# Low parts of every sixth weight granule by an accumulating DMA instead of a VectorE subtraction

## Chip, cores and metric

One core of a Trainium2 chip. The metric is the device time of one execution in microseconds (us), the median of three runs. A profile is one further execution with the hardware profiler on.

## What is computed

Two blocks of a hybrid network on 256 tokens of width 2048, all in float32: a convolution and sliding-window attention layer, then an indexer-selected attention layer and a stick-breaking attention layer, each with layer norms and gates. What matters here is that nearly all of it is products of 256 tokens with large weight matrices:

```python
proj = jnp.einsum("bsd,de->bse", x, w_in) + b_in                 # 2048 x 5376
y = jnp.einsum("bse,ed->bsd", y, w_out) + b_out                  # 2048 x 2048
h = x @ w_in_a                                                   # 2048 x 6224
(o * silu(g)) @ w_out_a ;  x @ w_ple_gate ;  p @ w_ple           # twice the last two
kb, vb = split(x @ w_kv_b) ;  q, g = split(x @ w_q_b)            # 2048 x 4096 each
(o * silu(g)) @ w_out_b
```

## The kernel before

Each weight matrix is cut into column chunks, each chunk into granules of 128 partitions x 1024 floats (512 KB; some are 768, 672 or 512 wide): four K-tiles of 256 columns or two of 512. `_plan()` fixes the order of all chunks, and `plan` the order of all 492 granules. For accuracy every float32 operand is split into a high part `hi`, rounded to float32r, and a low part `lo = raw - hi`. A product is then three products of parts: `gemm_T` (weights stationary, lines 338 and 339) takes `hi` against both parts of the activations in one 512-column matmul and `lo` against the high part in a 256-column one; `gemm` (activations stationary, lines 324 to 326) does the three one after the other.

A granule goes through four engines. `load` (lines 250 to 266) issues its DMA on SP's queue into the pool `wraw` of 6 buffers. `fetch` (268 to 278) has ScalarE (ACT) copy it to `hi` with rounding (line 277, the CAST rows), then VectorE (DVE) subtract (line 278, TENSOR_TENSOR); `hi` and `lo` come from the pools `whi` and `wlo` of 4 buffers each. `granules` (292 to 312) sets how far ahead this is written: when granule `here` is being multiplied, `hi` and `lo` of the next `AHEAD` = 2 are written and the next `LOAD` = 3 are loaded. A scheduling layer then orders each engine's instructions, within what buffers and data allow, so that ACT and DVE work further ahead than that. Each engine works its own queue in order. A `raw` buffer is free again when the subtraction has read it.

Attention, convolution and norms run beside this as generators (`side.pump()`, once per granule): small matmuls between the large ones, and ACT, DVE and GpSimd (POOL) work. POOL has little: masks (`affine_select`, line 231 and 1035) and two small DMAs (lines 831 and 835).

```python
            for p in plan[here:here + 1 + min(here, AHEAD)]:
                if p not in held:
                    held[p] = fetch(p)
```

Of the kernel before, what the change touches and what calls it, by code (L numbers as in the profile page):

```python
# [13 lines left out]
F32 = mybir.dt.float32  # L14
F32R = mybir.dt.float32r
I32 = mybir.dt.int32
AF = mybir.ActivationFunctionType
ALU = mybir.AluOpType
# [10 lines left out]
TAPS = 31  # L29
AHEAD = 2  # L30
LOAD = 3
PRE = 3
CONV_RATE = (3, 3)
BIG = 1e30
# [76 lines left out]
def _plan():  # L111

    w2 = [("w_in_a_2", key) for key in CHUNKS_2]
    parts = (("w_kv_b_2", "k", "xy"), ("w_q_b_2", "q", "xy"), ("w_kv_b_2", "v", ("",)), ("w_q_b_2", "g", "xy"))
    w3 = [(w, f"{n}{c}{h}") for c in range(4) for w, n, hs in parts for h in hs]
    square = lambda w: [(w, key) for key in CHUNKS_SQ]
    return [
        *[("w_in", key) for key in CHUNKS_1], *[("w_out", key) for key in CHUNKS_O1],
        ("w_ple0", "0"), ("w_ple0", "1"), *w2, *square("w_out_a_2"),
        ("w_ple0", "2"), ("w_ple0", "3"), *square("w_gate0"), *w3, *square("w_out_b_2"),  # L120
        *[("w_ple1", str(c)) for c in range(4)], *square("w_gate1"),
    ]


def _cols(ranges):
    return sum(n for _, n in ranges)


def _group(ranges, kts):

    if ranges == CHUNKS_1["gv0"][0]:
        return 1
    return min(len(kts), 4 if _cols(ranges) <= 256 else 2)
# [51 lines left out]
def tile_net(ctx: ExitStack, tc: tile.TileContext, t: dict, out: bass.AP):  # L185
    nc = tc.nc
# [5 lines left out]
    wraw = ctx.enter_context(tc.tile_pool(name="wraw", bufs=6))  # L192
    whi = ctx.enter_context(tc.tile_pool(name="whi", bufs=4))
    wlo = ctx.enter_context(tc.tile_pool(name="wlo", bufs=4))
    small = ctx.enter_context(tc.tile_pool(name="small", bufs=4))
    acc = ctx.enter_context(tc.tile_pool(name="acc", bufs=2, space=bass.MemoryType.PSUM))
    aux = ctx.enter_context(tc.tile_pool(name="aux", bufs=4, space=bass.MemoryType.PSUM))
# [5 lines left out]
    def uid(s):  # L203
        count[0] += 1
        return f"{s}_{count[0]}"

    def unit(shape=(P, 2, 512), dt=F32):

        return units.tile(list(shape), dt, tag="u", name=uid("u"))
# [20 lines left out]
    def keep(ap, base, cm, step, op, fill):  # L230
# [10 lines left out]
    held = {}  # L241
    plan = [
        (stream, key, g)
        for stream, key in _plan()
        for kts in (STREAMS[stream][key],)
        for g in range(0, len(kts[1]), _group(*kts))
    ]
    at = [0]

    loaded = {}  # L250

    def load(stream, key, g):

        ranges, kts = STREAMS[stream][key]
        n = _cols(ranges)
        kpg = _group(ranges, kts)
        src = t[stream]
        raw = wraw.tile([P, kpg * n], F32, tag="raw", name=uid("raw"))
        nc.sync.dma_start(
            raw,  # L260
            bass.AP(
                tensor=src.tensor, offset=src.offset + offsets[stream][key] + g * P * n,
                ap=[[kpg * n, P], [1, kpg * n]],
            ),
        )
        return raw

    def fetch(p, keep=False):

        raw = loaded.pop(p, None) or load(*p)  # L270
        shape = list(raw.shape)
        if keep:
            hi, lo = unit(shape, F32R), unit(shape, F32R)
        else:
            hi = whi.tile(shape, F32R, tag="hi", name=uid("whi"))
            lo = wlo.tile(shape, F32R, tag="lo", name=uid("wlo"))
        nc.scalar.copy(hi, raw)  # L277
        return hi, lo, nc.vector.tensor_tensor(lo, raw, hi.bitcast(F32), ALU.subtract)  # L278

    def prefetch(*wanted):  # L280

        for stream, key, count in wanted:
            kpg = _group(*STREAMS[stream][key])
            for g in range(0, count * kpg, kpg):
                p = (stream, key, g)
                if p not in held and plan.index(p) >= at[0]:
                    held[p] = fetch(p, True)
                yield
                yield

    def granules(stream, key, events):

        ranges, kts = STREAMS[stream][key]
        n = _cols(ranges)
        kpg = _group(ranges, kts)
        for g in range(0, len(kts), kpg):
            if events and g in events:
                events[g]()
            here = at[0]
            assert plan[here] == (stream, key, g)  # L300
            for p in plan[here:here + 1 + min(here, AHEAD)]:
                if p not in held:
                    held[p] = fetch(p)
            for p in plan[here:here + 1 + min(here, LOAD)]:
                if p not in held and p not in loaded:
                    loaded[p] = load(*p)
            hi, lo, pace = held.pop((stream, key, g))
            at[0] += 1
            for j in range(kpg):
                ws = slice(j * n, (j + 1) * n)  # L310
                yield kts[g + j], g + j == 0, g + j == len(kts) - 1, hi[:, ws], lo[:, ws]
            with tc.issue_after(pace.ins):
                side.pump()

    def gemm(stream, key, act, events=None):

        n = _cols(STREAMS[stream][key][0])
        both = acc.tile([P, 2, 512], F32, tag="acc", name=uid("acc"))
        ps = [both[:, tt, :] for tt in range(2)]
        for kt, first, last, wh, wl in granules(stream, key, events):  # L320
            for tt in range(2):
                ah, al = act(kt, slice(tt * P, (tt + 1) * P))
                o = ps[tt][:, :n]
                nc.tensor.matmul(o, ah, wh, start=first, stop=False)  # L324
                nc.tensor.matmul(o, ah, wl, start=False, stop=False)  # L325
                nc.tensor.matmul(o, al, wh, start=False, stop=last)  # L326
        return [p[:, :n] for p in ps]

    def gemm_T(stream, key, act, events=None):

        nf = _cols(STREAMS[stream][key][0]) // P
        ps = [acc.tile([P, 2, 2, S], F32, tag="acc", name=uid("acc")) for _ in range(nf // 2)]
        for kt, first, last, wh, wl in granules(stream, key, events):
            both, ah = act.both(kt), act(kt, slice(0, S))[0]
            for f in range(nf):
                o = ps[f // 2][:, f % 2]
                fs = slice(f * P, (f + 1) * P)
                nc.tensor.matmul(o, wh[:, fs], both, start=first, stop=False)  # L338
                nc.tensor.matmul(o[:, 0, :], wl[:, fs], ah, start=False, stop=last)  # L339
        return ps  # L340
# [419 lines left out]
    for c, (s, n) in enumerate(SPANS):  # L760
# [7 lines left out]
        if c == 0:  # L768
            ple[0] = Ple(0)
            side.add(prefetch(("w_ple0", "0", 1), ("w_ple0", "1", 1), ("w_in_a_2", "i0", PRE)), 1, "fetch")  # L770

    def block_end(i, yact, w_out, pre, final):

        ln = Norm(1 + i, z, t["ln_g_2"], t["ln_b_2"], i * D)
        for c, (s, n) in enumerate(SPANS):
# [7 lines left out]
            if c == 0:  # L783
                if i not in ple:
                    ple[i] = Ple(i)
                side.add(
                    prefetch(*[(f"w_ple{i}", str(p), 1) for p in pre], (f"w_gate{i}", "0", PRE)), 1, "fetch"
                )
# [378 lines left out]
```

## Time and profile before

| | us |
|---|---|
| median of 3 runs | 1455.53 (1455.53 to 1456.15) |
| the profiled execution | 1454.93 |
| its span, first to last instruction | 1453.2 |

The profiled execution is 0.60 below the median; 1.73 of its time lies around its span. The TensorE clock was granted at 0.999 of full speed. DMA moved 266 MB, 183 GB/s on average.

To read a profile like this, first look at which engine is busy over the whole span, then at what that engine waits for when it does not work. Work on the other engines counts only as far as that engine waits for it. A busy share is an average over stages, so the windows of the stages come next, and then the distance, in time, between an operand's being ready and its first use.

### The profile page before, as it was taken

What the parts mean: (1) busy time and instruction counts of PE and PEld (TensorE: products, weight loads), DVE (VectorE), ACT (ScalarE), POOL (GpSimd) and SP (SyncE); (2) the same over time, 40 slices, a digit from 0 to 9 for tenths busy, and PEclk for the clock granted to TensorE, in tenths of its full rate; (3) what the DMA queues carried; (4) which work ended last, traced back from release to release, by engine and by line L of the source; (5) the groups of instructions that cost most, each with busy time, mean ns of one, the idle gap of its engine ahead of it and who ended that gap; (6) DMA issues with size and microseconds to landing.
All of it is one profiled execution on the core that took longest, in us unless ns stands there. A gap on an engine that the chain in (4) does not pass through costs nothing.

```text
span 1453.2 us, 21296 instructions
## 1 busy us (share of the span) xinstructions
PE 1437.5 (99%) x8076; PEld 1243.4 (86%) x8076; DVE 1033.6 (71%) x1588; ACT 803.4 (55%) x1199; POOL 24.3 (2%) x51
## 2 busy tenths in 40 slices
PE   7999999999999999999999999999999999999998
PEld 6888888888997888888898898888888888889888
DVE  6999989998679966766758655555655555575754
ACT  6445778465545556646544445654655646554442
POOL 0000000000000000000000000100100001000000
PEclk9999999999999999999999999999999999999999
DMA  8755445556374655455764555555555555586462
GB/s 314 263 197 175 159 138 168 188 191 219 97 240 149 203 165 170 152 182 152 261 196 150 184 174 189 166 175 184 171 174 174 174 175 164 182 269 218 125 223 73
DMA packets 79798, 266.01 MB, mean 183 GB/s; under 512 B 9408, under 2 KB 10048, under 8 KB 79696
## 3 DMA queue, kind: packets, MB, share of 16 engines
q1 hardware_dynamic: 79632, 264.63, 56.3%
q8 instruction: 63, 1.03, 0.3%
q14 instruction: 39, 0.32, 0.1%
q0 software_dynamic: 64, 0.03, 0.0%
HBM read 262.53 MB, written 2.10 MB: 182 GB/s over the span
## 4 chain that ended last, share of the span: by engine, by line
PE 90%; DVE 6%; DMA 2%; issue 1%; ACT 1%; DVEq 0%; SPq 0%; ACTq 0%
PE acc L338 28%; PE acc L339 14%; PE acc L324 14%; PE acc L326 14%; PE acc L325 14%; DVE wlo L278 2%; DVE u L510 2%; DMA raw<-in_w_in 1%; PE o L603 1%; PE pt L384 1%; PE pT L579 1%; PE o L604 0%; DVE u L449 0%; DMA h<-in_ln_b 0%; PE z L1063 0%
## 5 line engine op out<-in xcount | busy, mean ns | idle before, releaser
L278 DVE TENSOR_TENSOR wlo<-raw,whi 128x1024 fp32r<-128x1024 f32 (+3 forms) x475 | 564.0, 1191 | 315.4 <-ACT whi L277 314.7
L277 ACT CAST whi<-raw 128x1024 fp32r<-128x1024 f32 (+3 forms) x475 | 485.8, 1026 | 518.8 <-PE acc L338 244.8
L338 PE MATMUL acc<-u,whi 128*128 128x512 f32 x2016 | 718.3, 400 | 7.7 <-DVE u L378 5.7
L339 PE MATMUL acc<-u,wlo 128*128 128x256 f32 x2016 | 566.9, 281 | 0.0
L338 PEld LDWEIGHTS acc<-u,whi 128*128 128x128 f32 x2016 | 379.4, 188 | 101.5 <-ACT whi L277 5.6
L339 PEld LDWEIGHTS acc<-u,wlo 128*128 128x128 f32 x2016 | 382.0, 189 | 0.3 <-DVE wlo L278 0.3
L324 PE MATMUL acc<-whi,u 128*128 128x512 f32 (+3 forms) x1004 | 358.7, 357 | 0.0
L325 PE MATMUL acc<-wlo,u 128*128 128x512 f32 (+3 forms) x1004 | 355.8, 354 | 0.5 <-DVE wlo L278 0.5
L326 PE MATMUL acc<-whi,u 128*128 128x512 f32 (+3 forms) x1004 | 355.5, 354 | 0.0
L324 PEld LDWEIGHTS acc<-whi,u 128*128 128x128 f32 x1004 | 189.7, 189 | 25.4 <-issue 1.7
L326 PEld LDWEIGHTS acc<-whi,u 128*128 128x128 f32 x1004 | 189.7, 189 | 25.3 <-DVE u L378 0.4
L325 PEld LDWEIGHTS acc<-wlo,u 128*128 128x128 f32 x1004 | 189.9, 189 | 24.4 <-DVE wlo L278 0.9
L510 DVE SCALAR_TENSOR_TENSOR u<-u,convw,u 128x255 f32<-128x255 f32 (+19 forms) x240 | 109.3, 466 | 3.9
L352 DVE TENSOR_TENSOR h<-acc,h 128x512 f32<-128x512 f32 x51 | 34.9, 685 | 5.5 <-ACT h L346 4.6
L467 DVE TENSOR_TENSOR u<-u,h 128x1024 f32<-128x1024 f32 x24 | 28.5, 1220 | 3.4 <-DMA h<-in_ln_g 3.4
L1035 POOL TENSOR_SCALAR_AFFINE_SELECT h<-h 128x256 f32<-128x256 f32 x32 | 18.1, 566 | 748.0 <-DVE h L1055 723.6
L377 ACT CAST u<-h 128x512 fp32r<-128x512 f32 (+1 forms) x32 | 18.0, 566 | 22.0 <-DVE h L616 15.6
L559 ACT ACTIVATE u<-u,negm 128x128 f32<-128x128 f32 x64 | 28.4, 446 | 2.6 <-DVE negm L551 2.6
L378 DVE TENSOR_TENSOR u<-h,u 128x512 fp32r<-128x512 f32 (+1 forms) x32 | 19.7, 622 | 13.9 <-ACT u L377 13.6
L346 ACT ACTIVATE h<-acc 128x512 f32<-128x512 f32 x42 | 24.9, 594 | 5.1 <-PE acc L339 3.8
L803 DVE TENSOR_TENSOR h<-h,u 128x512 f32<-128x512 f32 (+1 forms) x20 | 10.8, 582 | 20.8 <-ACT h L802 20.8
L277 ACT CAST u<-raw 128x1024 fp32r<-128x1024 f32 (+1 forms) x17 | 17.3, 1015 | 11.0 <-DMA raw<-in_w_ple 6.1
(197 smaller groups left out, 965.3 us busy)
## 6 DMA issues: line engine op xcount, KB each, us to landing
raw<-in_w_in_a SPq DMA_DIRECT2D x80, 512.0 KB, 3.6
raw<-in_w_in SPq DMA_DIRECT2D x76, 512.0 KB, 3.3
raw<-in_w_gate SPq DMA_DIRECT2D x64, 512.0 KB, 3.6
raw<-in_w_kv_b SPq DMA_DIRECT2D x64, 512.0 KB, 3.3
raw<-in_w_q_b SPq DMA_DIRECT2D x64, 512.0 KB, 3.3
raw<-in_w_out SPq DMA_DIRECT2D x32, 512.0 KB, 3.4
raw<-in_w_out_a SPq DMA_DIRECT2D x32, 512.0 KB, 4.2
raw<-in_w_out_b SPq DMA_DIRECT2D x32, 512.0 KB, 4.3
```

Of the source, the lines that this page charges most:

```text
L277: nc.scalar.copy(hi, raw)
L278: return hi, lo, nc.vector.tensor_tensor(lo, raw, hi.bitcast(F32), ALU.subtract)
L324: nc.tensor.matmul(o, ah, wh, start=first, stop=False)
L325: nc.tensor.matmul(o, ah, wl, start=False, stop=False)
L326: nc.tensor.matmul(o, al, wh, start=False, stop=last)
L338: nc.tensor.matmul(o, wh[:, fs], both, start=first, stop=False)
L339: nc.tensor.matmul(o[:, 0, :], wl[:, fs], ah, start=False, stop=last)
L346: nc.scalar.activation(t, ps[:, :, 1, :], AF.Copy, scale=scale)
L352: nc.vector.tensor_tensor(out_, ps[:, :, 0, :], t, ALU.add)
L467: nc.vector.tensor_tensor(self.z[c], self.z[c], r.unsqueeze(1).broadcast_to([P, 2, 512]), op)
L510: nc.vector.scalar_tensor_tensor(o[:, d:], h[:, :S - d], w, o[:, d:], ALU.mult, ALU.add)
L559: nc.scalar.activation(sc[:, i, cs], sc[:, i, cs], AF.Exp, bias=negm[:, i, tt:tt + 1], scale=-1.0, accum_out=den[:, i, tt:tt + 1],)
```

## The change

Of the granules of the plan, those with a number over 60 that divides by six, in the second half of their chunk (`g >= 8`), not within the last eight and not of `w_ple`, are `far`: 33 of the 492 (numbers 66, 78, 90, 132, 138, 156, 162, 168, 180, 192, ... 480). For a far granule `hi` and `lo` come from a pool of their own, `wfar`, with one buffer each. ACT writes `hi` by a copy and then (or first) `lo = -raw`, rounded to float32r, by an activation with scale -1. In place of the subtraction, POOL issues a DMA from `raw` to `lo`, SBUF to SBUF, that adds: `lo = raw - hi`. It is fetched 4 granules ahead in place of 2, and loaded 6 ahead in place of 3.

```diff
@@ -29,6 +29,7 @@
 AHEAD = 2
 LOAD = 3
+FAR, FAR_LOAD, FAR_STEP = 4, 6, 6
@@ -192,6 +193,7 @@
     wlo = ctx.enter_context(tc.tile_pool(name="wlo", bufs=4))
+    wfar = ctx.enter_context(tc.tile_pool(name="wfar", bufs=1))
@@ -265,12 +267,23 @@
+    def far(p):
+
+        i = plan.index(p)
+        return i > 60 and i % FAR_STEP == 0 and i < len(plan) - 8 and not p[0].startswith("w_ple") and p[2] >= 8
+
     def fetch(p, keep=False):
 
         raw = loaded.pop(p, None) or load(*p)
         shape = list(raw.shape)
         if keep:
             hi, lo = unit(shape, F32R), unit(shape, F32R)
+        elif far(p):
+            hi = wfar.tile(shape, F32R, tag="hi", name=uid("fhi"))
+            lo = wfar.tile(shape, F32R, tag="lo", name=uid("flo"))
+            nc.scalar.copy(hi, raw)
+            nc.scalar.activation(lo, raw, AF.Copy, scale=-1.0)
+            return hi, lo, nc.gpsimd.dma_start(lo.bitcast(F32), raw, accum_op=ALU.add)
         else:
             hi = whi.tile(shape, F32R, tag="hi", name=uid("whi"))
             lo = wlo.tile(shape, F32R, tag="lo", name=uid("wlo"))
@@ -298,11 +311,11 @@
             here = at[0]
             assert plan[here] == (stream, key, g)
-            for p in plan[here:here + 1 + min(here, AHEAD)]:
-                if p not in held:
+            for i, p in enumerate(plan[here:here + 1 + FAR]):
+                if p not in held and (i <= min(here, AHEAD) or far(p)):
                     held[p] = fetch(p)
-            for p in plan[here:here + 1 + min(here, LOAD)]:
-                if p not in held and p not in loaded:
+            for i, p in enumerate(plan[here:here + 1 + FAR_LOAD]):
+                if p not in held and p not in loaded and (i <= min(here, LOAD) or far(p)):
                     loaded[p] = load(*p)
```

The order of TensorE's matmuls stays as it was, but for a few transposes near granule 290. ACT's changes. This is ACT's queue at granule 322 in the stick-breaking stage, before: `whi_1630` is the high part of granule 322, `whi_1633` of 323, and the rows of lines 1066, 1071 and 609 are attention.

```order
L277 CAST whi_1630_9215<-raw_1623_9184 128x1024
L1071 CAST h_1615_9149<-h_1614_9146 128x256
L1066 ACTIVATE h_1619_9174<-z_1593_9046 128x384
L1071 CAST h_1620_9177<-h_1619_9174 128x256
L609 CAST u_1626_9208<-acc_1573_8959 128x512
L277 CAST whi_1633_9237<-raw_1632_9219 128x1024
```

And after the change, from the row that follows the same `whi_1630` on (lines after 312 are 13 higher); the row that follows the last one is the cast of `whi_1633`.

```order
L1079 ACTIVATE h_1614_9169<-z_1586_9036 128x384
L1084 CAST h_1615_9172<-h_1614_9169 128x256
L1079 ACTIVATE h_1619_9197<-z_1596_9075 128x384
L1084 CAST h_1620_9200<-h_1619_9197 128x256
L284 CAST fhi_1653_9381<-raw_1647_9337 128x1024
L285 ACTIVATE flo_1654_9382<-raw_1647_9337 128x1024
L1079 ACTIVATE h_1624_9225<-z_1603_9107 128x384
L622 CAST u_1626_9231<-acc_1573_8981 128x512
```

The two parts of far granule 330 (`fhi_1653`, `flo_1654`) now stand between the casts of granules 322 and 323, seven granules before their own place. Six of the 33 stand right behind the cast of the granule eight places before them like this one, nine behind that of the seventh before them, seven elsewhere, and eleven (90, 138, 162, 168, 234, 276, 348, 354, 444, 450, 480) behind that of the second before them, most of these because they wait for the single buffer of a far granule six places before.

This is SP's queue after the change, from the load of granule 326 (`raw_1641`) on: the load of far granule 330 (`raw_1647`) stands behind that of 327 and ahead of those of 328, 329 and 331. Before, these were in the order of their numbers.

```order
L261 DMA raw_1641_9308<-in_w_q_b_2 128x1024
L261 DMA raw_1646_9335<-in_w_q_b_2 128x1024
L261 DMA raw_1647_9337<-in_w_kv_b_2 128x1024
L261 DMA raw_1650_9359<-in_w_kv_b_2 128x1024
L261 DMA raw_1655_9386<-in_w_kv_b_2 128x1024
L261 DMA raw_1663_9433<-in_w_kv_b_2 128x1024
```

The far granule's load moved up by two places; it takes the buffer that the subtraction of granule 322 frees, and that load was granule 328's before.

This is POOL's queue after the change near granules 348 to 354, one of the places where the new DMAs stand among the masks of an attention group; `flo_1770` is far granule 354, and the AFFINE_SELECT rows on both sides of it followed each other directly before.

```order
L286 DMA flo_1728_9846<-raw_1719_9794 128x1024
L1048 AFFINE_SELECT h_1732_9870<-h_1732_9870 128x256
L1048 AFFINE_SELECT h_1739_9902<-h_1739_9902 128x256
L286 DMA flo_1770_10039<-raw_1759_9982 128x1024
L1048 AFFINE_SELECT h_1745_9932<-h_1745_9932 128x256
L1048 AFFINE_SELECT h_1753_9966<-h_1753_9966 128x256
```

The third and fourth mask of the group now stand behind a DMA that waits for ACT.

## Rows read from the trace of the kernel before

**Rows 1.** The page's first part: engine, busy us (share of span) xinstructions.

```profile
PE 1437.5 (99%) x8076; PEld 1243.4 (86%) x8076; DVE 1033.6 (71%) x1588; ACT 803.4 (55%) x1199; POOL 24.3 (2%) x51
```

**Rows 2.** Waits of TensorE: engine line <- releaser: us in total, times, longest.

```profile
PE acc L338 <- DVE u L378: 5.7, 1, 5.7
PE acc L338 <- DVE h L352: 2.0, 1, 2.0
PE pt L384 <- DVE h L352: 1.2, 1, 1.2
PE acc L324 <- DVE u L460: 0.5, 2, 0.3
PE acc L325 <- DVE wlo L278: 0.5, 1, 0.5
PE pt L384 <- ACT h L455: 0.3, 1, 0.3
```

**Rows 3.** Waits of the other engines, same columns.

```profile
DVE wlo L278 <- ACT whi L277: 314.7, 271, 3.5
...
ACT whi L277 <- PE acc L338: 244.8, 169, 2.8
ACT whi L277 <- PE acc L326: 226.2, 157, 7.2
```

**Rows 4.** TensorE's timeline, two stretches: start us, us, engine, line, operation.

```profile
879.85 0.39 PE L338 MATMUL acc<-u,whi 128*128 128x512 f32 x1
...
899.96 0.39 PE L338 MATMUL acc<-u,whi 128*128 128x512 f32 x1
...
971.23 0.40 PE L338 MATMUL acc<-u,whi 128*128 128x512 f32 x1
...
979.71 0.40 PE L338 MATMUL acc<-u,whi 128*128 128x512 f32 x1
```

**Rows 5.** Groups by form on DVE, then ACT: busy us, mean ns | idle before.

```profile
L278 DVE TENSOR_TENSOR wlo<-raw,whi 128x1024 fp32r<-128x1024 f32 x438 | 534.0, 1222 | 295.8 <-ACT whi L277 295.2
...
L277 ACT CAST whi<-raw 128x1024 fp32r<-128x1024 f32 x438 | 459.0, 1051 | 484.9 <-PE acc L338 242.4 <-PE acc L326 195.6 <-issue 25.3
```

**Rows 6.** Windows: stretch, length, busy us of PE, PEld, DVE, ACT, POOL, clock, DMA share, GB/s.

```profile
440.00:480.00 40.00, 39.49 (x208) 30.50 (x208) 37.22 (x86) 19.05 (x30) 1.81 (x2) 1.00 0.50 158
...
960.00:1000.00 40.00, 40.00 (x235) 35.05 (x234) 21.52 (x22) 20.58 (x25) 0.00 (x0) 1.00 0.53 173
```

**Rows 7.** DMA issues by line: count, KB each, median us from issue to landing.

```profile
raw<-in_w_kv_b SPq DMA_DIRECT2D x64, 512.0 KB, 3.3
...
raw<-in_w_out_b SPq DMA_DIRECT2D x32, 512.0 KB, 4.3
...
u<-in_x SPq DMA_DIRECT2D x8, 256.0 KB, 7.4
...
h<-in_inv POOLq DMA_DIRECT2D x1, 32.0 KB, 1.9
```

**Rows 8.** ACT's timeline at the casts of granules 322 and 323.

```profile
936.58 1.05 ACT L277 CAST whi<-raw 128x1024 fp32r<-128x1024 f32 x1
...
940.39 1.05 ACT L277 CAST whi<-raw 128x1024 fp32r<-128x1024 f32 x1
941.34 0.49 ACT L1066 ACTIVATE h<-z 128x384 f32<-128x384 f32 x1
```

**Rows 9.** DVE's timeline there: the subtraction of granule 322.

```profile
937.66 1.23 DVE L278 TENSOR_TENSOR wlo<-raw,whi 128x1024 fp32r<-128x1024 f32 x1 [0.94 <-ACT whi L277]
```

**Rows 10.** POOL's timeline near granule 350: the third mask of the group.

```profile
1027.16 0.41 POOL L1035 TENSOR_SCALAR_AFFINE_SELECT h<-h 128x256 f32<-128x256 f32 x1 [3.08 <-DVE h L1055]
```

**Rows 11.** TensorE's timeline there: attention products behind granule 348 and before 351.

```profile
1026.67 0.34 PE L1063 MATMUL z<-h,negtri 128*128 128x384 f32 x1
...
1033.33 0.34 PE L1063 MATMUL z<-h,negtri 128*128 128x384 f32 x1
```

## The prediction

> **What bounds the kernel now.** The page's first part comes first: TensorE is busy 1437.5 of 1453.2 us, DVE 71%, ACT 55%, POOL 2% [rows 1]. A busy TensorE could still be waiting inside its modelled ends, so the second view is its waits: they add up to 10.2 us, of which 7.7 are the two waits on L338 [rows 2]. The largest of these, 5.7 us for an activation, is the start of the kernel, ahead of any weight work that changes. On the line that this change takes work from, DVE's subtraction, TensorE waited once, 0.5 us. The third view says why: ACT's casts wait 471 us for TensorE to give a `whi` buffer back, and DVE's subtractions 315 us for ACT's casts [rows 3]. The supply of weights is held back by TensorE, not the other way round. The fourth view is TensorE's pace: 58 pairs of matmuls between 879.85 and 899.96 are 0.347 us a pair, 24 pairs between 971.23 and 979.71 are 0.353 [rows 4]. A granule of eight pairs is thus 2.8 us, and there are two paces, 2% apart, with no wait in them.
>
> The margin follows from this. A cast starts when TensorE is done with the granule four places before, so three granules (3 x 2.8 = 8.4) are left; the cast takes 1.05 and the subtraction 1.22 [rows 5], so low parts are ready about 6.1 us before use. In the indexer stage DVE is busy 37.2 of 40 us against 21.5 of 40 in a later one [rows 6], and the margin is thinner there.
>
> **The change, part by part.** All of it is off TensorE's queue; a term counts only where it uses up a margin.
>
> *Removed:* 33 subtractions, 33 x 1.22 = 40 us of DVE [rows 5]. DVE is not waited for but for 0.5 us, so this gives at most 0.5 us, in the crowded stage. I take all of it: -0.5. The waits on L352, L460 and L455 are norms and projections, which do not move.
>
> *Added on ACT:* 33 negations. No row shows one; the cast of the same tile, same engine, is 1.05 us [rows 5], so about 35 us on an engine that is 45% idle. By itself: 0.
>
> *ACT's order.* This is where a cost can arise. At granule 330 the far cast and negation stand between the casts of 322 and 323. The far load can start only when the subtraction of 322 has freed its buffer: that one ends at 937.66 + 1.23 = 938.9 [rows 9]. A 512 KB load lands 3.3 to 4.3 us later [rows 7], at 942.2 to 943.2, and ACT, working in order, stands still until then. Cast and negation take 2.1, the two attention instructions behind them about 1.1 (0.49 [rows 8] and one a little longer), so the cast of 323 starts at 945.4 to 946.4 in place of 940.39 [rows 8]: 5 to 6 us late against a margin of 6.1. Six far granules stand like this. The nine behind the seventh cast before them lose about one granule's time less, some 3 us, which the margin covers; after that ACT catches up at about 1 us a granule. If the load lands at 3.3 the cost is nothing. If it takes as long as the slowest kind of load here, 7.4 us [rows 7], the cast is 9.1 us late, 3.0 over the margin, six times: 18 us. Most loads are near the first figure; I take 0.3 us each: +1.8.
>
> *The adding transfer.* POOL issues 33 of them, each up to 512 KB from SBUF to SBUF. The trace has no such operation. From below: POOL's own 32 KB transfer lands in 1.9 us, a 512 KB load in 3.3 [rows 7]; it can hardly be quicker than the load. From above: the slowest kind of load, 256 KB in 7.4 us [rows 7], so 14.8 for 512 KB. An addition has to read `raw` and `lo` and write `lo`, twice the reading of a load; two loads of 3.6 plus issuing make 8 us, and I take 8, nearer the row of equal size. Against it stands the time left: for the 22 far granules written early that is more than 15 us. For the eleven written behind the second cast before them it is five granules, 14.0, less that cast and one or two operations of ACT: 10.9 to 11.9 us. At 8 us nothing is late: 0. At 14.8 each of the eleven is late by about 2.9: 32 us.
> For such a transfer from POOL's queue the Trainium skill (DMA: Bandwidth & Descriptors, Anatomy of one DMA) has a fit of 2.0 us plus bytes over 436 GB/s, which makes 3.2 us here as an estimate, or 4.4 with the bytes read twice. With that the sum would be the same and the margin wider. No run here shows it.
>
> *SP and `raw`.* A far `raw` is held until the transfer has landed, not until a subtraction has read it, so a load that takes its buffer, and SP's queue behind it, wait some 8 us longer than for a subtraction. The six buffers let loads land several granules before their casts; at 8 us this is covered, at 13 or more it adds to the late case.
>
> *POOL's order.* At granule 354 the third mask, at 1027.16 before [rows 10], stands behind a DMA that waits for a negation, and that waits for TensorE to end granule 348, about 1026.7 [rows 11]. Negation 1.05, the attention's own logarithm, a DVE step, the mask and the steps behind it (each 0.4 to 0.7, with the far cast of 1.05 between) end near 1030.5; the product that needs them starts at 1033.33 [rows 11]. 2.8 us in hand: 0. If issuing took longer than that, the cover is gone there.
>
> Sum: -0.5 + 1.8 = +1.3 on 1454.93 of the profiled execution, 1456.2; the median of the runs stood 0.6 above that execution, so **1456.8**. About 0.2%, 2.9 us, is what a measurement of this kernel can tell from no change, so this is "the same".
>
> **The rivals.**
>
> *The transfer is late (slower).* One mechanism: TensorE stands at the first matmul with a far `lo`. It decides from about 11 us from issue to landing. At 13 us it is eleven times 1.1 to 2.1, some 18 us, 1473; at 14.8 us 1488. For it: no row shows an adding transfer, the queue is shared with loads that keep the DMA engines half busy [rows 6]. Against it: every 512 KB row lands within 4.3.
> The Trainium skill (SBUF — State Buffer, Who interferes with whom) says that a DMA issued by GpSimd can be held up while DVE runs a copy, cast or one-input arithmetic in its two-port mode, because the descriptors are written through a port that the two share. That speaks against this change; it would lengthen the time from issue to landing. In rows, DVE's largest group is TENSOR_TENSOR [rows 5], which is not of that kind, so I leave this rival's chance nearly as it is. Chance 0.17.
>
> *ACT's detour costs more (slower).* As priced, a far load of 5 us or more in the six places: at 5 us 0.6 each, and a few us in the crowded stage at granule 180, where the margin is thinner; 4 to 10 us in all, 1460 to 1466. It decides where the cast behind the detour is over 6.1 us late. For it: the arithmetic above ends within a microsecond of the margin. Chance 0.20.
>
> *TensorE's pace changes (faster).* The two paces differ by 0.0067 us a pair, and there are 2016 pairs. If small waits at far granules, or other timing of the small matmuls between, put more stretches into the quicker pace, up to 13.4 us come back if all were slow now; 2.9 us need 440 pairs. Against it: the order of the matmuls stays, and nothing in the diff aims at this. 1450 to 1452. Chance 0.15, and 0.02 more that DVE's relief is worth more than its waits show.
>
> *The change does less than it says:* a far granule's work is only moved and nobody waits. That is the sum without its last term, 1455, inside "the same", 0.03.
>
> **How the numbers follow.** Forecast 0.43; with the last rival 0.46 for the same. Slower 0.17 + 0.20 = 0.37, faster 0.17. The likeliest case alone runs from 1453.5 to 1458.4. The range reaches down to 1451, which leaves out about 0.05 of the quicker pace, and up to 1471, which takes in the detour and leaves out the later half of the late transfers, about 0.1.
>
> **What would show it.** In the profile after: DVE's group on the subtraction smaller by 33 and its busy time near 994 us; ACT's near 838; 33 DMAs on POOL's queue landing in about 8 us; TensorE's waits still near 10 us with at most a few tenths on `flo`. A TensorE wait on `flo` of more than 3 us in all, with landings over 11 us, is the first rival. ACT waiting for a far `raw` for 3 us or more and TensorE then waiting for a `wlo` two to four granules later is the second. A time under 1452.6 with no wait gone and pairs at 0.347 in stretches that were at 0.353 is the third. The forecast is wrong if TensorE's waits grow by more than 3 us or the pace of its pairs shifts.

## The result: 7.8 us slower, and the profile after

The changed kernel takes 1463.62 us (median of 4 runs, 1461.64 to 1465.31) against 1455.84 before: ratio 1.0052, 95% interval 1.0040 to 1.0065. That is slower by more than the 0.2% that a measurement can tell. It lies inside the predicted range, but by luck: the upper part of the range stood for late transfers and for ACT's detour, and neither is what made this time. The likeliest case, 1456.8 and no difference, did not come.

The page's first part, with the same columns as [rows 1]:

```profile
PE 1442.7 (99%) x8076; PEld 1245.8 (85%) x8076; DVE 992.9 (68%) x1555; ACT 827.8 (57%) x1232; POOL 50.7 (3%) x84
```

The work moved as the diff says: DVE has 33 instructions and 41 us less, ACT 33 more and 24 us more, POOL issues 33 DMAs. (Neighbouring instructions overlap by about 0.1 us on ACT and count once, so its busy time grew by less than 33 x 1.05.) The span grew by 8.9 us, TensorE's busy time by 5.2. So some of the loss is waiting, and some is TensorE working more slowly. Its waits after, columns as in [rows 2] (lines of the changed kernel are 13 higher from line 312 on):

```profile
PE acc L351 <- DVE u L391: 5.8, 1, 5.8
PE ix L940 <- ACT h L943: 4.7, 1, 4.7
PE acc L351 <- DVE h L365: 2.0, 1, 2.0
PE acc L337 <- DVE u L473: 0.5, 2, 0.3
PE pt L397 <- ACT h L468: 0.3, 1, 0.3
PE pt L397 <- DVE u L817: 0.3, 1, 0.3
```

One large row is new: a single wait of 4.7 us at the index product L940, for an ACT operation (0.3 us at L397 for `u` is new too). The 0.5 us on DVE's subtraction and 1.2 us near the start (L384 before, at 113 us) are gone. Nothing waits for `flo`. In all the waits grew from 10.2 to 13.6 us. The groups of the new instructions (busy us, mean ns | idle before, by releaser), and two rows of the DMA issues (count, KB, median us to landing):

```profile
L284 ACT CAST fhi<-raw 128x1024 fp32r<-128x1024 f32 (+1 forms) x33 | 34.1, 1033 | 16.7 <-DMA raw<-in_w_q_b 8.0
L285 ACT ACTIVATE flo<-raw 128x1024 fp32r<-128x1024 f32 (+1 forms) x33 | 34.6, 1047 | 6.4 <-PE acc L338 6.4
L286 POOL DMA_DIRECT2D flo<-raw x33 | 28.9, 876 | 1105.1 <-ACT flo L285 976.1
```

```profile
raw<-in_w_kv_b SPq DMA_DIRECT2D x64, 512.0 KB, 3.9
...
flo<-raw POOLq DMA_DIRECT2D x31, 512.0 KB, 5.2
```

The adding transfer lands in 5.2 us in the median, well within its time. To find where the loss is, the start of each TensorE matmul is compared with the start of the matmul of the same number before (the order is the same but for a few small transposes). The difference in us, at times of the trace before, for this kernel and for those of the experiments below:

```
time before    after   e11    e2    e9    e1   e10    e5    e6
        120    +1.01 +1.07 +0.39 +1.71 +1.78 +3.64 +1.43 +0.89
        420    +1.10 +1.13 +0.34 +1.68 +2.15 +3.71 +1.47 +0.97
        450    +8.44 +9.39 +5.94 +2.51 +2.15 +3.71 +1.48 +0.97
        480    +7.63 +8.59 +5.13 +2.78 +1.42 +2.91 +0.67 +0.16
        510    +7.63 +8.49 +5.03 +2.77 +2.51 +2.91 +0.71 +0.06
        end    +8.69 +8.25 +5.37 +2.83 +2.97 +3.76 +0.88 +0.60
```

The first microsecond or more lies ahead of 120 us, where no far granule has been used; e6, which has none at all, shows it too. The loss is one step of 7.3 us between 420 and 450; behind it the column moves by a microsecond at most, as that of e6 does. The timelines show how it comes about. SP's queue there, before and then after (start us, us, grouped; a row lasts as long as SP stands at it):

```profile
418.05 0.33 SPq L259 DMA_DIRECT2D raw<-in_w_in_a  x1
418.43 0.43 SPq L405 DMA_DIRECT2D h<-in_ln_g  x1
```

```profile
415.48 11.78 SPq L261 DMA_DIRECT2D raw<-in_w_in_a  x4
427.31 1.43 SPq L418 DMA_DIRECT2D h<-in_ln_g  x1
```

The four raw loads take 11.78 us in which SP mostly stands. SP's waits in the window from 415 to 445 name what it stood for, and the tile `flo` from 415 to 430 how long that transfer took:

```profile
SPq L261 <- DMA flo<-raw: 7.3, 1, 7.3
```

```profile
DMA to landing us min/median/max: 7.7/7.7/7.7
```

This is the load of granule 159. It takes the buffer that the raw weights of far granule 156 hold until their adding transfer, issued at 419.19, has landed. Behind it in SP's queue stand four norm rows (gain and shift, issued by `row()`). They are issued 8.9 us later than before (1.1 of it because TensorE was already that far behind). Before, DVE waited 0.22 us for the first of these rows, so they had no slack (in brackets the idle time before and what ended it):

```profile
424.02 1.23 DVE L467 TENSOR_TENSOR u<-u,h 128x1024 f32<-128x1024 f32 x1 [0.22 <-DMA h<-in_ln_g]
```

Then DVE, ACT and TensorE, after, one timeline each:

```profile
425.26 1.23 DVE L291 TENSOR_TENSOR wlo<-raw,whi 128x1024 fp32r<-128x1024 f32 x1 [0.30 <-ACT whi L290]
432.39 1.22 DVE L480 TENSOR_TENSOR u<-u,h 128x1024 f32<-128x1024 f32 x1 [5.91 <-DMA h<-in_ln_g]
```

```profile
440.50 1.05 ACT L290 CAST whi<-raw 128x1024 fp32r<-128x1024 f32 x1 [6.14 <-DVE h L365]
444.48 0.62 ACT L984 CAST u<-h 128x512 fp32r<-128x512 f32 x1 [2.93 <-DVE h L892]
445.00 0.40 ACT L988 COPY h<-h 128x256 f32<-128x256 f32 x1
445.31 1.62 ACT L943 ACTIVATE h<-ix 128x384 f32<-128x384 f32 x4
```

```profile
440.87 0.28 PE L352 MATMUL acc<-u,flo 128*128 128x256 f32 x1
445.84 0.96 PE L940 MATMUL ix<-kiT,u 64*128 64x128 f32 x3 [4.70 <-ACT h L943]
...
447.80 0.79 PE L351 MATMUL acc<-u,whi 128*128 128x512 f32 x1
```

DVE stands 5.91 us for a norm row, ACT then stands for DVE, and TensorE for ACT, which has to read earlier index products (`h<-ix`) first. The last row shows the second part of the loss: a matmul of 128x512 takes 0.79 us, not 0.40. The windows (length, PE busy, granted clock, DMA share, GB/s) say why:

```profile
436.00:441.00 5.00, 5.00 (x32) 1.00 0.92 358
441.00:443.00 2.00, 0.15 (x2) 1.00 0.76 274
...
444.00:446.00 2.00, 0.16 (x1) 0.56 0.23 94
446.00:451.00 5.00, 5.00 (x18) 0.50 0.80 239
451.00:456.00 5.00, 5.00 (x28) 0.99 0.85 184
```

The granted clock falls to 0.50, the 1.2 GHz level, at 444.3, still within the wait, and is back at 1.00 at 451.1. In the 5.2 us of this that lie behind the wait TensorE does about half its work: 18 matmuls in 5 us from 446, against 32 in the 5 us ahead of the wait. Half of 5.2 is 2.6 us, and with the wait of 4.7 that is the step of 7.3.

### The profile page after: what moved, and what is told of

The parts are those of the page before. It is cut to its first block, busy times and chain, and to the rows that moved or that the text cites. A ratio compares the mean times of both kernels' runs of the same rounds, so it can differ in the third digit from the quotient of the medians.

```text
span 1462.1 us, 21329 instructions
## 1 busy us (share of the span) xinstructions
PE 1442.7 (99%) x8076; PEld 1245.8 (85%) x8076; DVE 992.9 (68%) x1555; ACT 827.8 (57%) x1232; POOL 50.7 (3%) x84
## 4 chain that ended last, share of the span: by engine, by line
PE 93%; DMA 2%; DVE 2%; ACT 1%; issue 1%; POOL 0%; SPq 0%; DVEq 0%; ACTq 0%
PE acc L351 31%; PE acc L352 16%; PE acc L337 14%; PE acc L339 13%; PE acc L338 13%; PE o L616 1%; PE pt L397 1%; PE pT L592 1%; DMA raw<-in_w_in 1%; DMA flo<-raw 1%; PE o L617 0%; DMA h<-in_ln_g 0%; DVE u L462 0%; DMA raw<-in_w_q_b 0%; ACT whi L290 0%
## 5 line engine op out<-in xcount | busy, mean ns | idle before, releaser
L291 DVE TENSOR_TENSOR wlo<-raw,whi 128x1024 fp32r<-128x1024 f32 (+3 forms) x442 | 522.9, 1189 | 306.1 <-ACT whi L290 305.1
L290 ACT CAST whi<-raw 128x1024 fp32r<-128x1024 f32 (+3 forms) x442 | 450.4, 1024 | 475.1 <-PE acc L351 225.2
L351 PE MATMUL acc<-u,whi 128*128 128x512 f32 x1880 | 673.9, 402 | 7.8 <-DVE u L391 5.8
L352 PE MATMUL acc<-u,wlo 128*128 128x256 f32 x1880 | 529.6, 282 | 0.0
L337 PE MATMUL acc<-whi,u 128*128 128x512 f32 (+3 forms) x932 | 332.4, 357 | 0.0
L339 PE MATMUL acc<-whi,u 128*128 128x512 f32 (+3 forms) x932 | 329.5, 354 | 0.0
L286 POOL DMA_DIRECT2D flo<-raw x33 | 28.9, 876 | 1105.1 <-ACT flo L285 976.1
L351 PE MATMUL acc<-u,fhi 128*128 128x512 f32 x136 | 49.3, 402 | 0.0
L284 ACT CAST fhi<-raw 128x1024 fp32r<-128x1024 f32 (+1 forms) x33 | 34.1, 1033 | 16.7 <-DMA raw<-in_w_q_b 8.0
L285 ACT ACTIVATE flo<-raw 128x1024 fp32r<-128x1024 f32 (+1 forms) x33 | 34.6, 1047 | 6.4 <-PE acc L338 6.4
L352 PE MATMUL acc<-u,flo 128*128 128x256 f32 x136 | 38.2, 281 | 0.0
```

The lines of the kernel that those rows point to most:

```text
L285: nc.scalar.activation(lo, raw, AF.Copy, scale=-1.0)
L286: return hi, lo, nc.gpsimd.dma_start(lo.bitcast(F32), raw, accum_op=ALU.add)
```

## Experiments

**Theory A**: the load of 159 waits on SP for the adding transfer of 156, the norm rows behind it are late, and DVE, ACT and TensorE stand in turn. **Rivals**: B, the far casts and negations on ACT delay TensorE in many places; C, the transfers slow other transfers everywhere; D, chance in TensorE's pace or clock. Each kernel is the changed one with the edit shown; ratios are to the kernel before.

**e1: without granule 156**

```diff
-        return i > 60 and i % FAR_STEP == 0 and i < len(plan) - 8 and not p[0].startswith("w_ple") and p[2] >= 8
+        return i > 60 and i % FAR_STEP == 0 and i != 156 and i < len(plan) - 8 and not p[0].startswith("w_ple") and p[2] >= 8
```

> The changed kernel with 32 of its 33 far granules: granule 156 is formed as before, by DVE. Theory A (the load of granule 159 stands on SP behind the adding transfer of 156, and the norm rows behind it come 8 us late): TensorE's 4.7 us wait at the index product (L940) and the half clock behind it are gone; 7.3 us less than the changed kernel, 1455.5 to 1457.5, within 0.2% of before. Rival B (the far casts and negations on ACT delay TensorE here and there) and rival C (33 transfers slow other transfers everywhere): 32 of 33 causes remain, so 1462 to 1464. Rival D (chance: the slow pace of TensorE, or its clock alone): stays near 1463, with the clock falling somewhere.

1457.28 us, ratio 1.0013 (1.0003 to 1.0023). The wait at L940 is gone, and no step is left between 420 and 450. One of 33 far granules carries most of the cost. About 1.4 us stay, against A's "within 0.2%" no contradiction, but more than nothing.

**e2: only granule 156**

```diff
-        return i > 60 and i % FAR_STEP == 0 and i < len(plan) - 8 and not p[0].startswith("w_ple") and p[2] >= 8
+        return i == 156 and i < len(plan) - 8 and not p[0].startswith("w_ple") and p[2] >= 8
```

> The kernel before with one far granule, 156, and none of the other 32. A: the whole cost is here, 1461 to 1464, with a TensorE wait of 4 to 5 us at L940 and SP blocked about 8 us at 419. B and C: one of 33 causes, at most 0.3 us: 1455.5 to 1456.3. D: 1455.5 to 1463 by chance, without a wait of TensorE at L940.

1460.81 us, ratio 1.0039 (1.0025 to 1.0052). Its SP row, DVE row and TensorE row at the place:

```profile
414.73 11.92 SPq L261 DMA_DIRECT2D raw<-in_w_in_a  x4
426.70 0.42 SPq L418 DMA_DIRECT2D h<-in_ln_g  x1
```

```profile
431.13 1.23 DVE L480 TENSOR_TENSOR u<-u,h 128x1024 f32<-128x1024 f32 x1 [5.40 <-DMA h<-in_ln_g]
```

```profile
444.01 0.48 PE L940 MATMUL ix<-kiT,u 64*128 64x128 f32 x2 [3.61 <-ACT h L943]
```

A as predicted in kind; the wait is 3.6 us against 4 to 5 expected, and the time is 0.2 us under its bound of 1461. The granted clock fell here too (mean 0.83 from 440 to 450). B and C are out as the main cause.

**e3: five norm rows on ACT's queue**

```diff
     def row(src, at, n):
+        q = nc.scalar if 150 < seen[0] < 156 else nc.sync
         r = short((P, n))
-        nc.sync.dma_start(
+        q.dma_start(
```

(`seen[0]` is the granule that TensorE has come to in the program.)

> The changed kernel, all 33 far granules, but the first five norm rows of the stage (four gain and shift rows and the next) are issued from ACT's queue in place of SP's, so that they do not stand behind the load of 159. A: SP still stands some 8 us before that load, but the rows land on time, DVE does not stand at L480 for them, TensorE's 4.7 us wait is gone: 1456 to 1458. If it is the late load itself (weights of 159 late) and not the rows: 1462 to 1464, with a TensorE wait at a weights line. B, C, D: 1462 to 1464.

1458.32 us, ratio 1.0017 (1.0008 to 1.0025). Every transfer is kept and the large wait is gone. Its bound of 1458 was passed by 0.3 us: TensorE waits 1.0 us for a low part at 459 (see e8).

**e4: far granules with DVE's subtraction**

```diff
-            nc.scalar.activation(lo, raw, AF.Copy, scale=-1.0)
-            return hi, lo, nc.gpsimd.dma_start(lo.bitcast(F32), raw, accum_op=ALU.add)
+            return hi, lo, nc.vector.tensor_tensor(lo, raw, hi.bitcast(F32), ALU.subtract)
```

> The changed kernel with its far order and its own pool, but each far low part is formed by DVE's subtraction from raw and high part, as before: no negation, no transfer. A: raw is freed by a subtraction of 1.2 us in place of a transfer of 5 to 8, SP does not stand: 1455.5 to 1457. B, if it is the far cast's place in ACT's order: 1460 to 1463; if it is the negations' 35 us: 1456. C (the transfers load the DMA engines): 1456. D: 1463 or 1456 by chance.

1457.77 us, ratio 1.0016 (1.0007 to 1.0025): between A's figure and B's. With raw freed by a subtraction the step at 440 is gone; 1.9 us stay that are neither negation nor transfer. The trace shows a TensorE wait of 1.6 us at the score product L556, at 503; e1 has one at the same product, which e10 follows up.

**e5: other far granules, 154 and 160 in place of 156**

```diff
-        return i > 60 and i % FAR_STEP == 0 and i < len(plan) - 8 and not p[0].startswith("w_ple") and p[2] >= 8
+        return i > 60 and i % FAR_STEP == 4 and i < len(plan) - 8 and not p[0].startswith("w_ple") and p[2] >= 8
```

> The changed kernel with other far granules: those whose number leaves 4 when divided by 6, so 154 and 160 in place of 156; 34 in all. The four norm rows then stand on SP behind a load that waits for a subtraction, not for a transfer. A: no stall at 419 to 450, no TensorE wait at L940, 1455.5 to 1458. If the cost came with far granules as such in this stage: 1461 to 1464.

1456.15 us, ratio 0.9998 (0.9990 to 1.0007). Far granules in the same stage, with the same transfers, cost nothing that can be measured. SP there:

```profile
418.07 0.42 SPq L418 DMA_DIRECT2D h<-in_ln_g  x1
```

The rows are issued on time, as before.

**e6: the pool, but no far granule**

```diff
-        return i > 60 and i % FAR_STEP == 0 and i < len(plan) - 8 and not p[0].startswith("w_ple") and p[2] >= 8
+        return i < 0 and i < len(plan) - 8 and not p[0].startswith("w_ple") and p[2] >= 8
```

> The changed kernel with its pool for far tiles but no far granule at all. The three kernels without the stall stood 0.13 to 0.17% over before. If that rest is the work of the 32 other far granules: 1455.5 to 1456.3, the same as before. If it is where tiles lie in memory (the pool moves them) or TensorE's pace at the start, which no far granule touches: 1457 to 1458.

1456.00 us, ratio 1.0000 (0.9991 to 1.0009). The pool's line costs nothing. No tile is taken from it here, so this run does not test where tiles lie; e5, which takes them, costs nothing either. So what e1, e3 and e4 keep belongs to their far granules. TensorE's waits in e6, all that the view lists:

```profile
PE acc L351 <- DVE u L391: 5.1, 1, 5.1
PE acc L351 <- DVE h L365: 2.4, 1, 2.4
PE acc L337 <- DVE u L473: 0.5, 2, 0.3
PE pt L397 <- ACT h L468: 0.3, 1, 0.3
```

In its trace TensorE, DVE, ACT and SP run the same instructions in the same order as in the trace of the kernel before. Still, the 0.5 us wait for a low part at 463 and the 1.2 us wait at 113 are not there. Waits of this size come and go without the change.

**e7: e1 with each transfer done twice** (the raw weights are added twice)

```diff
+            nc.gpsimd.dma_start(lo.bitcast(F32), raw, accum_op=ALU.add)
             return hi, lo, nc.gpsimd.dma_start(lo.bitcast(F32), raw, accum_op=ALU.add)
```

> The kernel of e1 with every one of its 32 adding transfers done twice, one behind the other (the raw weights are added twice, so the low parts are not the reference's). C: if the transfers' load on the DMA engines costs the 1.4 us that e1 stands over before, 1458.5 to 1459.5. If they are hidden: the same as e1, 1456.5 to 1458, as long as the second lands in time; the eleven with the short margin of 10.9 to 11.9 us may then make TensorE wait on a far low part, 1 to 3 us each, which would show as waits at the line of the low product and give up to 1475.

1482.21 us, ratio 1.0174 (1.0160 to 1.0187), above the bound of 1475. This is what late transfers look like:

```profile
PE acc L339 <- DMA flo<-raw: 5.8, 4, 3.6
...
PE acc L353 <- DMA flo<-raw: 4.8, 2, 4.0
PE acc L339 <- DVE wlo L292: 3.3, 5, 0.9
```

TensorE waits 10.6 us for far low parts in six places, and its mean clock falls to 0.993. So the margin against a late transfer is real: one transfer of 5 us fits into it, two in a row do not. Whether the load of the DMA engines costs anything (C) can't be read from this run, since lateness covers it.

**e8: e2 with the transfer done twice, norm rows ahead** (156's raw weights are added twice; the doubled transfer moves the rows ahead of the load of 159)

```diff
-        return i > 60 and i % FAR_STEP == 0 and i < len(plan) - 8 and not p[0].startswith("w_ple") and p[2] >= 8
+        return i == 156 and i < len(plan) - 8 and not p[0].startswith("w_ple") and p[2] >= 8
...
+            nc.gpsimd.dma_start(lo.bitcast(F32), raw, accum_op=ALU.add)
             return hi, lo, nc.gpsimd.dma_start(lo.bitcast(F32), raw, accum_op=ALU.add)
```

> The kernel of e2 (156 the only far granule) with its adding transfer done twice (low part of 156 wrong), which makes the order put the four norm rows ahead of the load of 159 on SP. A: the transfer takes twice as long and still nothing stalls at L940, since the rows no longer stand behind a load that waits for it: 1455.5 to 1457. If the far granule itself, its transfer or its negation in this stage is what costs: as e2 or more, 1460.8 to 1466.

1461.06 us, ratio 1.0031 (1.0020 to 1.0043). My expectation missed: the time lies where the far granule itself would cost, and not only the rows' place. The wait at the index product is down to 0.4 us, as A has it, but TensorE waits 2.8 us for another low part, up to 461, and the granted clock is then 0.50 for 3.4 us. DVE and TensorE there:

```profile
439.77 1.22 DVE L292 TENSOR_TENSOR wlo<-raw,whi 128x1024 fp32r<-128x1024 f32 x1
...
448.31 1.22 DVE L481 TENSOR_TENSOR u<-u,h 128x1024 f32<-128x1024 f32 x1 [3.36 <-DMA h<-in_ln_g]
...
459.80 1.22 DVE L292 TENSOR_TENSOR wlo<-raw,whi 128x1024 fp32r<-128x1024 f32 x1
```

```profile
461.07 0.54 PE L339 MATMUL acc<-wlo,u 128*128 128x512 f32 x1 [2.82 <-DVE wlo L292]
```

The subtraction that ends the wait stands in DVE's queue behind the next norm, which itself waits 3.36 us for its row, and behind index work. From 439.77 to 459.80 DVE starts no subtraction; in the kernel before it starts three in that stretch (441.62, 452.88 and 456.14). The changed kernel, e2, e3 and e9 have such a gap too (17 to 18 us, ending between 458 and 462), while e1, e5, e6 and e10 have subtractions between 451 and 457. So DVE's order with 156's low part made by a transfer looks like a second and smaller cost in this stage: TensorE waits there in e3, e8 and e9, and in e2 and the changed kernel, where it is already late, it does not. No run moved this order alone, so this is read from the traces and not shown by an experiment. The run did not tell the theories apart. e9 was built to move one thing.

**e9: the load of 159 behind the norm rows**

```diff
-                    loaded[p] = load(*p)
+                    with tc.issue_after(rows[ROWS - 1].ins) if plan.index(p) == 159 else nullcontext():
+                        loaded[p] = load(*p)
```

(`rows` lists the DMAs that `row()` has issued and `ROWS` is 8; the eighth is the last of these four. The lines that fill the list are left out here. On SP one load changes place, on DVE four subtractions move behind the next norm step; no other engine's order changes, but for one index product near 442 that starts a place earlier in the trace.)

> The changed kernel with all 33 far granules and their transfers; the one change is that the load of granule 159 is put behind the four norm rows in SP's queue (four subtractions of DVE move by one or two places with it, nothing else). Theory A: SP stands before that load as before, but the rows land at 424 to 426, TensorE's 4.7 us wait at L940 and the half clock after it are gone: 1456 to 1458.5, where up to 1.5 us may stay for the later norm rows or for the far cast of 180. If it is the far granule itself, its transfer or ACT's order at 156: 1461 to 1465.

1457.49 us, ratio 1.0013 (1.0004 to 1.0022), beside 1.0046 for the changed kernel on the same chip (e11). SP and DVE:

```profile
416.06 4.06 SPq L264 DMA_DIRECT2D raw<-in_w_in_a  x3
420.17 0.50 SPq L422 DMA_DIRECT2D h<-in_ln_g  x1
```

```profile
428.22 1.23 DVE L484 TENSOR_TENSOR u<-u,h 128x1024 f32<-128x1024 f32 x1 [2.68 <-DMA h<-in_ln_g]
```

All 33 far granules and transfers are there, and the step of 7.3 us is 0.8. A holds: the cost is the order of one load and four rows on one queue. The rows, expected at 424 to 426, landed only at 428.2: 8 us from issue, with 156's transfer (8.2 us in this run) under way at the same time; before, the first took 5.6 us (418.43 to 424.0). The median landing of the two gain rows is 8.2 us here, 7.3 before and 6.1 in e1 and e6, which have no such transfer. C may have a small part there; this was not separated. Behind the step TensorE waits another 0.8 us at 459, for a subtraction that stands late in DVE's queue as in e8: DVE starts none from 440.63 to 458.69.

**e10: e1 without granule 180 too**

```diff
-        return i > 60 and i % FAR_STEP == 0 and i != 156 and i < len(plan) - 8 and not p[0].startswith("w_ple") and p[2] >= 8
+        return i > 60 and i % FAR_STEP == 0 and i != 156 and i != 180 and i < len(plan) - 8 and not p[0].startswith("w_ple") and p[2] >= 8
```

> The kernel of e1 with granule 180 not far either. In e1 and e4 the far cast of 180 stands on ACT for its raw weights (4.25 us in e1), the casts behind it are late, DVE waits 2.5 us for one, and TensorE waits 1.1 us for a score operand: the detour of ACT that the prediction priced. If that is the 1.4 us by which e1 stands over before: 1455 to 1456.5, no TensorE wait at L557. If the 1.4 us come from the other far granules or from chance: 1457 to 1458.

1456.15 us, ratio 1.0004 (0.9995 to 1.0013). In e1 the far cast of 180 stands on ACT for its raw weights, and the ordinary casts behind it with it; TensorE then waits for an operand that ACT makes later:

```profile
490.42 1.05 ACT L284 CAST fhi<-raw 128x1024 fp32r<-128x1024 f32 x1 [4.25 <-DMA raw<-in_w_in_a]
491.37 1.05 ACT L285 ACTIVATE flo<-raw 128x1024 fp32r<-128x1024 f32 x1
492.33 1.98 ACT L290 CAST whi<-raw 128x1024 fp32r<-128x1024 f32 x2
```

```profile
504.69 0.49 PE L557 MATMUL s<-h,h 128*128 128x128 f32 x2 [1.08 <-ACT h L988]
```

In e10 that wait is not there. Over the kernel before, measured beside each, e1 stands 1.4 us and e10 0.8. The difference of 0.6 us is less than the wait, and their intervals overlap: the trace shows this cause, the times alone do not.

**e11: the changed kernel again**, without an edit

> The changed kernel as it is, beside e9 and e10 on one chip. A: 1462 to 1465 with the same 4 to 5 us wait of TensorE at L940 in this execution, since it follows from the order of SP's queue and not from chance. D (chance): the wait or the half clock is gone in this execution, or the median falls below 1460.

1462.24 us (5 runs, 1461.35 to 1464.32), ratio 1.0046 (1.0034 to 1.0059), with the wait again:

```profile
PE ix L940 <- ACT h L943: 5.2, 1, 5.2
```

D is out: the stall follows from the order of the queue.

No version beats the kernel before: the best, e5, e6 and e10, can't be told from it.

## Why the prediction was wrong in its likeliest case

- **What bounds the kernel: right. What DVE's relief gives: not shown.** The subtractions were hidden, and DVE came to 992.9 us, predicted 994. The one wait for them, priced at -0.5, is gone, and TensorE gains 0.7 us there (463.7 us before; from +8.44 to +7.77). But e6, in which DVE does every subtraction, lacks this wait too and gains 0.8 us between 450 and 480. The gain is not shown to come from the relief.
- **Negations: right.** 1.047 us each, hidden. ACT's busy time was predicted as 838 and is 827.8.
- **The adding transfer: right, the duration too long.** 5.2 us in the median (4.4 to 8.9) against 8 taken; no wait for `flo`, as forecast. e7 shows what the first rival would have cost: two transfers in a row give 26 us over before. The rival's text put the transfers and the loads on one queue; the page after lists two (q0 with the transfers, q1 with the loads), so what they share is the DMA engines. The estimate from the Trainium skill's fit (DMA: Bandwidth & Descriptors, Anatomy of one DMA), 3.2 us, or 4.4 with the bytes read twice, was nearer than my 8; the measured 5.2 lies above both. That DVE could hold such a DMA up (the Trainium skill, SBUF — State Buffer, Who interferes with whom) no row here shows; why some transfers took 8.9 us was not tried.
- **SP and `raw`: this is the step that failed.** The text said that a load which takes a far buffer, "and SP's queue behind it", wait some 8 us longer, and "at 8 us this is covered". The hold was as said (7.7 us), and TensorE did not wait for the weights of 159. But I asked only when the next weights are needed, not what else stands behind that load on SP. Four norm rows stood there, with no slack, for a stage in which DVE is nearly full [rows 6]. Priced 0, it measured 7.3 us in the trace: 4.7 us of wait, and the rest in the stretch at half clock behind it. By the prediction's own sign, TensorE's waits growing by more than 3 us, the forecast was wrong: they grew by 3.4. My own method would have caught it: every load that takes a far buffer, and the rows behind it on SP, 33 places to look up.
- **The clock was in no term.** I priced waits at their length. Here one of 4.7 us brought 7.3.
- **ACT's detour: right in kind, and small.** +1.8 were taken for six places, and TensorE waited at none of them; the rival's text also named granule 180, and e1 shows 1.1 us there. In the changed kernel itself it did not show: after the stall the loads were ahead of ACT, and the far cast of 180 stood only 0.22 us. The second rival's times, 1460 to 1466, held the result, but its mechanism was not what made it.
- **POOL's order at granule 354: right**, no wait of TensorE there.
- **TensorE's pace: no gain.** The first 120 us, ahead of any far granule, differed by 0.4 to 3.6 us between traces of kernels that are alike there, which is chance; part of it is the clock, as the last section shows.
- What stays open: of the 0.13 to 0.17% that e1, e3, e4 and e9 keep, e10 explains 1.1 us of e1's by the trace, and e4 has the like at the same product. In e3 and e9 it is TensorE waits of 0.8 to 1.0 us for a low part near 460. The traces put them down to DVE's order there (e8), which no run changed by itself.

## What to carry to other kernels

When a change lengthens the time for which a buffer is held, look up on the loading queue what stands behind the load that takes that buffer: the queue is in order, and the small urgent transfer behind the large patient one pays. Moving one load behind four small rows (e9) took away some 5 of 7 us; choosing other granules (e5) took away all of it. And a new wait of some microseconds on TensorE is to be priced with the slower clock that may follow it.

## What was not expected of the hardware

- After, or already within, a TensorE wait of 3.6 us (e2), 4.7 (the changed kernel) and 5.2 (e11) the granted clock fell to half, for 3.4, 6.8 and 6.8 us. It fell after 2.8 us in e8 too, for 3.4 us; after the wait of 1.1 us in e1 it stayed at 1.00. The step in the matmuls' starts was larger than the wait by 2.0 (e2), 2.6 and 3.1 us.
- The length of the wait alone does not decide it. At about 30 us, ahead of any far granule, TensorE waits 1.8 to 3.1 us in every trace; a few us later the clock was 0.50 for 3.4 us in seven of them (e1, e2, e5, e7, e9, e10, e11) and 1.00 in the other six. The same window in e10 and then in the kernel before (waits of 3.1 and 2.0 us):

```profile
36.00:38.00 2.00, 2.00 (x8) 0.50 1.05 406
```

```profile
36.00:38.00 2.00, 2.00 (x13) 1.00 1.03 379
```

- The accumulating transfer of 512 KB within SBUF lands in 5.2 us in the median, beside 3.5 to 4.8 for the weight loads of that size in the same execution, and costs POOL 0.88 us to issue.
- Two such transfers of one tile, one behind the other (e7), did not double their own landing time (5.8 us each in the median), yet took 25 us of the kernel's time, since the second starts only when the first has landed.
